# Two more places in a ring of split weights, paid with two of seven slab row buffers

## The chip, the cores and the metric

One core of one Trainium2 chip runs the whole program. The metric is the device time of one execution in microseconds, where lower is better. In the text PE is TensorE (PEld its weight loads), DVE is VectorE, ACT is ScalarE, POOL is GpSimd and SP is SyncE, which here only issues DMAs.

## The reference

Two decoder layers over 256 tokens of width 2048, in float32. Layer 0 mixes tokens by causal pooling and by attention to a memory of 256 tokens, layer 1 by differential attention over shared keys and values and by the same memory attention. Both end with a squared-ReLU feed-forward part (FFN) of width 8192, and these two FFNs are where the change acts:

```python
def squared_relu_mlp(h, w1, w2):
    z = jax.nn.relu(h @ w1)
    return (z * z) @ w2
...
        x = x + jnp.concatenate([token_out, mem_out], axis=-1) @ w_out[i]
        x = x + squared_relu_mlp(rms_norm(x, ffn_norm[i]), w_ff1[i], w_ff2[i])
```

## The kernel before, in words

The matmuls run in a rounded float32 format. To keep float32 accuracy every operand is split into a high part (the rounded value) and a low part (the rest), and a product is the sum of high times high, low times high and high times low. All weights (some 370 MB) pass through once: a DMA brings a row of 128x1024 from memory, ACT casts the high part (line 178), DVE subtracts it and gets the low part (line 181), and PE uses both. This supply is the class `Feed`.

The high and low parts lie in a ring of places of 512 columns: six in `hi_ring`/`lo_ring`, and during an FFN two more in the tile `slot` (`feed.extra`). `_slots` hands out one or two adjacent places and never goes across the end of a section, so a pair that does not fit skips a place. `fill(job)` prepares jobs up to `AHEAD` = 3 beyond the one that PE takes next, as long as places are free; `free(job)` returns them.

An FFN has two kinds of jobs. An up tile (64 a layer, `narrow`, lines 942 and 944) multiplies one column block of `w_ff1` into the single bank `x_bank`; it takes two plain rows (`R` jobs, two places each). The down product runs for half of its columns (A) and the other half (B) in 7 phases (`PHASES`), by a scheme with seven products in place of eight, whose seven PSUM banks are called `p`. It takes slabs, 58 a layer: a slab is two rows of `w_ff2`, to the first of which POOL adds part of the second by a summing DMA (line 149); DVE forms further sums in place (lines 209 and 212), and four jobs of 2, 1, 2 and 2 places come of it (`run`, lines 1033 to 1035, three matmuls for each place). `ffn_plan` mixes the two: up to two slab jobs ahead of an up tile for the first two tiles of a phase, then four or five. At a phase's end `finish_banks` takes the banks down on ACT and DVE, adds the sums of an earlier phase by a gather on POOL's queue (line 1089) or parks them in memory on SP's (line 1093). Eight last down tiles (`down_tile`) close the FFN.

Rows need buffers. Plain rows have four (`raw`). Slab rows have the three buffers `rows` and during an FFN also the room of the residual, whose four quarters are stored to memory first (`kept`, line 855): seven buffers in turn (`feed.more`). Quarters a and b are out of that turn from the next to last slab of phase 5 (the last B phase), c and d later. In phase 6 (the last A phase, the tail below) the residual comes back by `reload` (line 862): a and b after slab 23, c and d after slab 31.

In the tail there is more to do beside the slabs: the results of phase 5 are turned (transposes named `ct`) and added to the residual (line 1105), and in the end so are those of phase 6.

The instructions of each engine run in the order in which a scheduler has put them, which knows the places, the buffers and estimated durations. So a change of the ring also changes how casts, copies and DMAs stand in their queues.

Of the kernel before, what the change touches and what calls it, by code (L numbers as in the profile page):

```python
# [10 lines left out]
F32 = mybir.dt.float32  # L11
F32R = mybir.dt.float32r
# [6 lines left out]
P = 128  # L19
T = 256  # L20
# [6 lines left out]
SLOTS, AHEAD, LOADS, KOFF, RAWS = 6, 3, 3, 2, 4  # L27
# [78 lines left out]
class Feed:  # L106


    def __init__(self, tc, wst, wpool, rows, plan, dry):
        self.tc, self.nc, self.wst, self.wpool, self.rows = tc, tc.nc, wst, wpool, rows  # L110
        self.plan, self.dry = plan, dry
        self.pos = 0
        self.slab_no = 0
        self.lp = self.pp = 0
        self.raw = {}
        self.split = {}
        self.rows_whole = False
        self.extra = None
        self.more, self.lent, self.turn = [], {}, 0
        if not dry:  # L120
            self.hi = wpool.tile([P, SLOTS * 512], F32R, name="hi_ring")
            self.lo = wpool.tile([P, SLOTS * 512], F32R, name="lo_ring")
            self.busy = [False] * (SLOTS + 2)
            self.at = 0

    def load(self, upto):
# [26 lines left out]
            self.lp += 1  # L153

    def _slots(self, n):
        total = SLOTS + 2 if self.extra else SLOTS
        a = self.at
        if a < SLOTS < a + n:
            a = SLOTS
        if a + n > total:  # L160
            a = 0
        if any(self.busy[a : a + n]):
            return None
        for i in range(a, a + n):
            self.busy[i] = True
        self.at = a + n
        return a

    def _split(self, job, src, n):
        a = self._slots(n)  # L170
        if a is None:
            return False
        if a < SLOTS:
            hi, lo = self.hi[:, a * 512 : (a + n) * 512], self.lo[:, a * 512 : (a + n) * 512]
        else:
            c = (a - SLOTS) * 512
            hi, lo = (self.extra[:, b + c : b + c + n * 512] for b in (0, 1024))
        cast = self.nc.scalar.copy(hi, src)  # L178
        if self.pp < 2 or job[0] == "S" and job[2] == 0:
            self.tc.keep_in_program_order(cast)  # L180
        self.nc.vector.tensor_sub(lo, src, hi.bitcast(F32))  # L181
        self.split[job] = (hi, lo, range(a, a + n))
        return True
# [34 lines left out]

    def fill(self, job):
        i = self.plan.where[job]  # L220
        while self.pp < min(i + 1 + AHEAD, len(self.plan.prep)):
            if not self._prepare(self.plan.prep[self.pp]):
                assert self.pp > i
                break
            self.pp += 1
# [68 lines left out]
NB = 26  # L294
# [3 lines left out]
LAST = len(PHASES) - 1  # L298
# [67 lines left out]
def program(ctx, tc, plan, dry, xT, memT, par, lam, cst, wst, yT):  # L366
    nc = tc.nc
    cp = ctx.enter_context(tc.tile_pool(name="cp", bufs=1))
    sp = ctx.enter_context(tc.tile_pool(name="sp", bufs=1))
# [7 lines left out]
    feed = Feed(tc, wst, wp, tp, plan, dry)  # L377
# [7 lines left out]
    def at(d, fn, rank=0):  # L385
        pend.setdefault(now[0] + d, []).append((rank, fn))
# [33 lines left out]

    memraw = sp.tile([P, NK, T], F32, tag="S1", name="memraw")
    def resid_part(i, name):
        return sp.tile([P, 4, T], F32, tag=f"resid{i}", name=name)

    resid = Halves([resid_part(i, f"resid{i}") for i in "abcd"], 4)
    gmem = cp.tile([P, NK], F32, name="gmem")
    nc.scalar.dma_start(gmem, par[:, G_MEM : G_MEM + NK])

# [408 lines left out]
    def ffn(l, xs, tag, done):  # L837
# [7 lines left out]
        feed.extra = None if dry else sp.tile([P, 2048], F32R, tag="half", name=f"slot{l}")  # L845
# [7 lines left out]
        kept = dp.tile([P, NK, T], F32, tag="kept", name=f"kept{l}")  # L853
# [3 lines left out]
        def reload(tags):  # L857
            for i in tags:
                assert f"resid{i}" not in feed.lent.values()
                j = "abcd".index(i)  # L860
                resid.parts[j] = resid_part(i, f"resid{i}{l}")
                nc.sync.dma_start(resid.parts[j], kept[:, 4 * j : 4 * j + 4, :])

        feed.more = [] if dry else [(sp, f"resid{i}") for i in "abcd"]
        spare = list(range(len(spots)))
        zat, sat, due = {}, {}, {}

        def take():
            return spare.pop(0)
# [179 lines left out]
        def finish_banks(p):  # L1049

            half, begin, end = PHASES[p]
# [60 lines left out]
            if p == LAST:  # L1112
                for t, side in enumerate((upp, low)):
                    stt(
                        side, side, r2c[0][:, t : t + 1], fetched[t].bitcast(F32),
                        ALU.mult, ALU.add,
                    )
                for h in range(4):
                    at(7 + h, lambda h=h: turn(h))
                return  # L1120
            if old is not None:
                at(10, gather)
# [16 lines left out]
        ends = [None]  # L1139

        def go(some):
            for at_, what in some:
                if what[0] == "s":
                    p, i, j = what[1:]
                    if not banks:
                        open_banks()
                    if (p, i) not in runs:
                        runs[p, i] = slab_jobs(p, i)
                    runs[p, i](j)
                    if at_ < first_down and at_ >= ups:  # L1150
# [44 lines left out]
    half = sp.tile([P, 2048], F32R, tag="half", name="half0")  # L1195
# [295 lines left out]
    ab = [carve(384) for _ in range(2)]  # L1491
# [167 lines left out]
    for c in range(3):  # L1659
# [5 lines left out]
        for i in range(2):  # L1665
            j = 2 * c + i
# [127 lines left out]
```

## Time and profile before

| | |
|---|---|
| median of 3 runs | 2031.41 us (2030.1 to 2033.28) |
| the profiled execution's own time | 2031.04 us |
| its span, first to last instruction | 2029.3 us |
| granted PE clock | 1.000 of full speed |
| DMA | 453.43 MB, mean 223 GB/s |
| FFN of layer 0, FFN of layer 1 | from about 240 to 935 us, from about 1325 to 2025 us |

The two FFNs are over two thirds of the span. A group's row gives the line, the engine, what is written from what, how often, the busy time and the mean of one, and then the idle time of the engine just before, with what ended it. A row of the waits gives the engine and line that waited, the one waited for, and then the total in us, the number of waits and the longest. A row of the timeline gives start and duration in us. A row of the windows gives the stretch, its length, and the busy time of PE, PEld, DVE, ACT and POOL with the number of instructions, then the granted clock, the DMA engines' busy share and GB/s.

### The profile page before, as it was taken

The page shows a single profiled execution, that of the slowest core. Times are in us where ns is not written, and L with a number is a line of the kernel's source. Part 1 is how long each engine was busy: PE and PEld are TensorE (multiplying, and loading weights), DVE is VectorE, ACT ScalarE, POOL GpSimd, SP SyncE. Part 2 cuts the span into 40 slices and gives each one's busy share as a digit, 9 for nine tenths or more (in the row PEclk, how much of TensorE's full clock was granted, in tenths as well). Part 3 has the DMA queues.
Part 4 walks back from the last instruction along what each step waited for, and adds up shares of the span by engine and source line. Part 5 has one row for each costly group of instructions (what it writes and reads, how often), then busy time and mean ns, then how long its engine had stood idle before and what let it go on. Part 6 is the DMA issues. An engine that isn't in the chain of part 4 may idle for free.

```text
span 2029.3 us, 30490 instructions
## 1 busy us (share of the span) xinstructions
PE 2013.5 (99%) x10548; PEld 1695.9 (84%) x10548; DVE 1797.7 (89%) x2713; ACT 1376.7 (68%) x2213; POOL 175.0 (9%) x207
## 2 busy tenths in 40 slices
PE   9999999999999999999999999999999999999999
PEld 7888888888888888788888899888888888888877
DVE  8888779999999999999875798879999989898989
ACT  7765567666666676668665698566676667676764
POOL 0001300001011111000000000410001001010100
PEclk9999999999999999999999999999999999999999
DMA  9566767778788788765655645767877878786874
GB/s 309 181 199 214 238 202 246 243 219 262 221 237 261 238 244 235 239 190 194 222 185 191 194 141 181 237 225 230 238 229 223 263 223 269 214 265 214 260 205 156
DMA packets 139978, 453.43 MB, mean 223 GB/s; under 512 B 15856, under 2 KB 18928, under 8 KB 139824
## 3 DMA queue, kind: packets, MB, share of 16 engines
q1 hardware_dynamic: 119520, 412.68, 60.6%
q0 software_dynamic: 20160, 38.81, 11.5%
q8 instruction: 82, 1.34, 0.3%
q14 instruction: 72, 0.59, 0.1%
q10 hardware_dynamic: 144, 0.01, 0.0%
HBM read 431.90 MB, written 16.78 MB: 221 GB/s over the span
## 4 chain that ended last, share of the span: by engine, by line
PE 94%; DVE 3%; ACT 1%; issue 1%; DMA 1%; SPq 0%; DVEq 0%; ACTq 0%
PE x_bank L942 21%; PE x_bank L944 11%; PE p L1033 9%; PE p L1035 8%; PE p L1034 8%; PE wo L521 6%; PE wo L523 3%; PE ff L942 3%; PE q L552 3%; PE k L552 3%; PE v L552 3%; PE u L521 2%; PE mk L552 2%; PE mv L552 2%; PE ff L944 1%; DVE lo_ring L181 1%
## 5 line engine op out<-in xcount | busy, mean ns | idle before, releaser
L181 DVE TENSOR_TENSOR lo_ring<-raw,hi_ring 128x512 fp32r<-128x512 f32 (+1 forms) x657 | 551.8, 852 | 92.9 <-ACT hi_ring L178 86.7
L178 ACT CAST hi_ring<-raw 128x512 fp32r<-128x512 f32 (+1 forms) x657 | 480.4, 744 | 212.1 <-PE wo L521 62.3
L178 ACT CAST hi_ring<-slab 128x1024 fp32r<-128x1024 f32 (+1 forms) x350 | 312.9, 905 | 180.2 <-DVE slab L212 156.9
L181 DVE TENSOR_TENSOR lo_ring<-slab,hi_ring 128x1024 fp32r<-128x1024 f32 (+1 forms) x350 | 361.6, 1046 | 46.2 <-ACT hi_ring L178 44.6
L149 POOL DMA_DIRECT2D slab<-in_w x116 | 100.3, 865 | 1632.0 <-DVE rc L496 338.5
L942 PE MATMUL x_bank<-fx,hi_ring 128*128 128x512 f32 x688 | 218.7, 396 | 1.0 <-ACT hi_ring L178 0.9
L181 DVE TENSOR_TENSOR slot<-slab,slot 128x1024 fp32r<-128x1024 f32 x114 | 139.4, 1223 | 28.0 <-ACT slot L178 23.7
L521 PE MATMUL wo<-cat,hi_ring 128*128 128x512 f32 x512 | 161.7, 397 | 0.0
L944 PEld LDWEIGHTS x_bank<-fx,lo_ring 128*128 128x128 f32 x688 | 129.0, 188 | 30.8 <-DVE lo_ring L181 1.2
L178 ACT CAST slot<-slab 128x1024 fp32r<-128x1024 f32 x114 | 119.7, 1050 | 40.5 <-PE x_bank L942 31.5
L212 DVE TENSOR_TENSOR slab<-slab,slab 128x1024 f32<-128x1024 f32 x116 | 141.8, 1222 | 0.3
L944 PE MATMUL x_bank<-fx,lo_ring 128*128 128x256 f32 x688 | 136.2, 279 | 0.0
L942 PE MATMUL x_bank<-fx0b,hi_ring 128*128 128x512 f32 x384 | 120.7, 396 | 0.0
L523 PEld LDWEIGHTS wo<-cat,lo_ring 128*128 128x128 f32 x512 | 96.2, 188 | 21.9
L942 PEld LDWEIGHTS x_bank<-fx,hi_ring 128*128 128x128 f32 x688 | 107.9, 189 | 6.0 <-ACT hi_ring L178 2.1
L1033 PE MATMUL p<-hi_ring,zb 128*128 128x512 f32 x274 | 109.7, 401 | 1.3 <-ACT hi_ring L178 1.1
L1035 PE MATMUL p<-lo_ring,zb 128*128 128x512 f32 x274 | 106.2, 397 | 1.7 <-DVE lo_ring L181 1.7
L1034 PE MATMUL p<-hi_ring,zb 128*128 128x512 f32 x274 | 107.0, 392 | 0.0
L956 ACT COPY room<-x_bank 128x512 f32<-128x512 f32 x118 | 68.5, 580 | 49.6 <-PE x_bank L944 49.5
L523 PE MATMUL wo<-cat,lo_ring 128*128 128x256 f32 x512 | 101.8, 278 | 0.0
L942 PE MATMUL x_bank<-fx0a,hi_ring 128*128 128x512 f32 x304 | 97.7, 396 | 0.5 <-ACT hi_ring L178 0.2
L178 ACT CAST slot<-raw 128x1024 fp32r<-128x1024 f32 (+1 forms) x72 | 73.8, 1028 | 29.7 <-PE x_bank L942 16.5
(554 smaller groups left out, 4773.7 us busy)
## 6 DMA issues: line engine op xcount, KB each, us to landing
raw<-in_w SPq DMA_DIRECT2D x492, 512.0 KB, 4.5
slab<-in_w SPq DMA_DIRECT2D x232, 512.0 KB, 4.4
slab<-in_w POOLq DMA_DIRECT2D x116, 256.0 KB, 5.8
part<-room SPq DMA_DIRECT2D x10, 512.0 KB, 4.4
room<-part POOLq DMA_DIRECT2D x8, 512.0 KB, 10.1
part<-c_x SPq DMA_DIRECT2D x10, 256.0 KB, 5.6
part<-c_y SPq DMA_DIRECT2D x10, 256.0 KB, 4.6
c_x<-part POOLq DMA_DIRECT2D x8, 256.0 KB, 5.8
```

The source lines that it names most:

```text
L149: self.nc.gpsimd.dma_start(t[:, 512:1024], self.wst[other, :, 512:1024], accum_op=ALU.add)
L178: cast = self.nc.scalar.copy(hi, src)
L181: self.nc.vector.tensor_sub(lo, src, hi.bitcast(F32))
L212: add(two, t.unsqueeze(1).to_broadcast([P, 2, 512]), two)
L521: nc.tensor.matmul(ps, hi, xs[:, k, :], start=first and j == 0, stop=False)
L523: nc.tensor.matmul(ps[:, T : 2 * T], lo, xs[:, k, 0:T], start=False, stop=last and j == len(ks) - 1,)
L552: nc.tensor.matmul(ps[t], a, b, start=i == 0 and j == 0, stop=i == NK - 1 and j == 2)
L942: nc.tensor.matmul(ps, hi, src(k), start=k == ks[0], stop=False)
L944: nc.tensor.matmul(ps[:, T : 2 * T], lo, src(k)[:, 0:T], start=False, stop=k == ks[-1])
L1033: nc.tensor.matmul(ps, al, hi[:, s], start=i == begin, stop=False)
L1034: nc.tensor.matmul(ps, ah, hi[:, s], start=False, stop=False)
L1035: nc.tensor.matmul(ps, ah, lo[:, s], start=False, stop=i == end - 1)
```

## The change

The quarters a and b of the residual's room become one tile `resida`. In an FFN it is a second `slot` of two places, so the ring has ten. `ahead` is 5 during the FFN. Slab rows have the turn of `rows` and quarters c and d alone: five buffers. After slab 22 of phase 5 the new places are taken out of use again; a and b are reloaded after slab 22 of phase 6 (as two DMAs into one tile), the turn of c and d ends after slab 27 and not 28, and the turns at the very end of the FFN stand one tick later.

```diff
     def _slots(self, n):
-        total = SLOTS + 2 if self.extra else SLOTS
+        ends = range(SLOTS, SLOTS + 2 * len(self.extra) + 1, 2)
         a = self.at
-        if a < SLOTS < a + n:
-            a = SLOTS
-        if a + n > total:
+        for end in ends:
+            if a < end < a + n:
+                a = end
+        if a + n > ends[-1]:
             a = 0
...
-        while self.pp < min(i + 1 + AHEAD, len(self.plan.prep)):
+        while self.pp < min(i + 1 + self.ahead, len(self.plan.prep)):
...
     def resid_part(i, name):
-        return sp.tile([P, 4, T], F32, tag=f"resid{i}", name=name)
+        if i == "a":
+            both = sp.tile([P, 8, T], F32, tag="resida", name=name)
+            return [both[:, 0:4, :], both[:, 4:8, :]]
+        return [sp.tile([P, 4, T], F32, tag=f"resid{i}", name=name)]
...
-        feed.more = [] if dry else [(sp, f"resid{i}") for i in "abcd"]
+        feed.more = [] if dry else [(sp, f"resid{i}") for i in "cd"]
+        feed.ahead = 5
...
+        feed.extra = [] if dry else [
+            sp.tile([P, 2048], F32R, tag=tag, name=f"slot{l}") for tag in ("half", "resida")
+        ]
...
-                    at(7 + h, lambda h=h: turn(h))
+                    at(8 + h, lambda h=h: turn(h))
...
-                    if (p, i, j) == (LAST - 1, NB - 2, 3):
-                        feed.more = feed.more[2:]
-                    if (p, i, j) == (LAST, 23, 3):
-                        reload("ab")
-                    if (p, i, j) == (LAST, 28, 3):
+                    if (p, i, j) == (LAST - 1, 22, 3):
+                        del feed.extra[1:]
+                    if (p, i, j) == (LAST, 22, 3):
+                        assert dry or not any(feed.busy[SLOTS + 2 :])
+                        reload("a")
+                    if (p, i, j) == (LAST, 27, 3):
                         feed.more = []
...
                 if at_ == len(items) - 3:
-                    feed.extra = None
+                    feed.extra = []
+                    feed.ahead = AHEAD
```

How the instructions move, at two places. The number behind `raw` or `slab` is that of the weight row in the order of the stream; the last number only tells buffers apart. First ACT at the end of phase 2 in layer 0, from the copy of the first bank of that phase (`c_x<-p0`) to the copy of the up tile's bank (`x_bank`) and on. Before:

```order
L1066 COPY c_x_4498<-p0_3742 128x512
L925 CAST za0_2624<-room0_2626 128x512
L1067 COPY room0_2626<-p6_3748 128x512
L178 CAST hi_ring_76<-slab169_4360 128x1024
L178 CAST slot0_2627<-raw173_4472 128x1024
L178 CAST hi_ring_76<-raw174_4477 128x1024
L956 COPY room0_2626<-x_bank_4510 128x512
L178 CAST hi_ring_76<-slab169_4360 128x512
L178 CAST hi_ring_76<-slab170_4380 128x1024
```

And of the change at the same place:

```order
L1074 COPY c_x_4503<-p0_3746 128x512
L180 CAST hi_ring_76<-slab169_4350 128x1024
L180 CAST slot0_2631<-raw173_4447 128x1024
L1075 COPY room0_2625<-p6_3752 128x512
L180 CAST hi_ring_76<-slab169_4350 128x512
L180 CAST slot0_2632<-raw174_4468 128x1024
L180 CAST hi_ring_76<-slab170_4356 128x1024
L964 COPY room0_2625<-x_bank_4515 128x512
```

Two casts of slab rows that stood behind the copy of `x_bank` stand ahead of it. Next SP's queue in layer 0, at the reload of the residual's quarter a (b follows) shortly ahead of the tail. Before:

```order
L147 DMA slab300_7194<-in_w 128x1024
L147 DMA slab303_7274<-in_w 128x1024
L147 DMA raw297_7132<-in_w 128x1024
L147 DMA raw298_7170<-in_w 128x1024
L862 DMA resida0_7387<-kept0_2628 128x1024
L147 DMA raw301_7204<-in_w 128x1024
L147 DMA raw302_7272<-in_w 128x1024
L862 DMA residb0_7389<-kept0_2628 128x1024
```

And of the change, from the same reload on:

```order
L866 DMA resida0_7303<-kept0_2626 128x1024
L148 DMA slab287_6873<-in_w 128x1024
L148 DMA raw291_6956<-in_w 128x1024
L148 DMA slab289_6951<-in_w 128x1024
L148 DMA raw292_7032<-in_w 128x1024
L866 DMA resida0_7303<-kept0_2626 128x1024
L148 DMA slab290_6954<-in_w 128x1024
L148 DMA raw293_7034<-in_w 128x1024
L148 DMA raw294_7036<-in_w 128x1024
L148 DMA slab295_7046<-in_w 128x1024
```

The reload moves some ten weight rows ahead, and the slab rows stand less far ahead of the plain rows: 303 is issued ahead of 297 before, 295 behind 294 in the change.

More of the change, by code (lines that the diff above doesn't have):

```diff
@@ L117, in __init__ @@
         self.rows_whole = False
-        self.extra = None
+        self.extra = []
+        self.ahead = AHEAD
         self.more, self.lent, self.turn = [], {}, 0
@@ L122, in __init__ @@
             self.lo = wpool.tile([P, SLOTS * 512], F32R, name="lo_ring")
-            self.busy = [False] * (SLOTS + 2)
+            self.busy = [False] * (SLOTS + 4)
             self.at = 0
@@ L175, in _split @@
         else:
-            c = (a - SLOTS) * 512
-            hi, lo = (self.extra[:, b + c : b + c + n * 512] for b in (0, 1024))
+            which, c = divmod((a - SLOTS) * 512, 1024)
+            hi, lo = (self.extra[which][:, b + c : b + c + n * 512] for b in (0, 1024))
         cast = self.nc.scalar.copy(hi, src)
@@ L422, in resid_part @@
     def resid_part(i, name):
-        return sp.tile([P, 4, T], F32, tag=f"resid{i}", name=name)
-    resid = Halves([resid_part(i, f"resid{i}") for i in "abcd"], 4)
+        if i == "a":
+            both = sp.tile([P, 8, T], F32, tag="resida", name=name)
+            return [both[:, 0:4, :], both[:, 4:8, :]]
+        return [sp.tile([P, 4, T], F32, tag=f"resid{i}", name=name)]
+    resid = Halves([x for i in "acd" for x in resid_part(i, f"resid{i}")], 4)
     gmem = cp.tile([P, NK], F32, name="gmem")
@@ L844, in ffn @@
         room = sp.tile([P, 4096], F32, tag="big", name=f"room{l}")
-        feed.extra = None if dry else sp.tile([P, 2048], F32R, tag="half", name=f"slot{l}")
         feed.rows_whole = True
@@ L859, in reload @@
                 assert f"resid{i}" not in feed.lent.values()
-                j = "abcd".index(i)
-                resid.parts[j] = resid_part(i, f"resid{i}{l}")
-                nc.sync.dma_start(resid.parts[j], kept[:, 4 * j : 4 * j + 4, :])
-        feed.more = [] if dry else [(sp, f"resid{i}") for i in "abcd"]
+                for j, x in enumerate(resid_part(i, f"resid{i}{l}"), "abcd".index(i)):
+                    resid.parts[j] = x
+                    nc.sync.dma_start(x, kept[:, 4 * j : 4 * j + 4, :])
+        feed.more = [] if dry else [(sp, f"resid{i}") for i in "cd"]
+        feed.ahead = 5
         spare = list(range(len(spots)))
         zat, sat, due = {}, {}, {}
+        feed.extra = [] if dry else [
+            sp.tile([P, 2048], F32R, tag=tag, name=f"slot{l}") for tag in ("half", "resida")
+        ]
         def take():
```

## The prediction

> **What bounds the kernel now.** I read the head of the profile's page first, then the waits of the weight loads, then TensorE's timeline at one stop, and last the queues that feed it.
>
> ```profile
> span 2029.3 us, 30490 instructions
> PE 2013.5 (99%) x10548; PEld 1695.9 (84%) x10548; DVE 1797.7 (89%) x2713; ACT 1376.7 (68%) x2213; POOL 175.0 (9%) x207
> ```
>
> TensorE (PE) is busy for all but 15.8 us. A matmul's row lasts longer than the step to the next one, though, so short stops are swallowed. They show in the starts. A stretch of an up tile, a stop, and ScalarE (ACT) at that stop:
>
> ```profile
> 475.54 0.63 PE L942 MATMUL x_bank<-fx0a,slot 128*128 128x512 f32 x2
> 476.00 0.39 PE L944 MATMUL x_bank<-fx0a,slot 128*128 128x256 f32 x2
> 476.23 0.63 PE L942 MATMUL x_bank<-fx0a,slot 128*128 128x512 f32 x2
> ...
> 481.33 0.39 PE L1034 MATMUL p<-hi_ring,zb 128*128 128x512 f32 x1
> 481.56 0.39 PE L1035 MATMUL p<-lo_ring,zb 128*128 128x512 f32 x1
> 481.97 0.73 PE L942 MATMUL x_bank<-fx0a,slot 128*128 128x512 f32 x2
> 482.54 0.44 PE L1033 MATMUL p<-hi_ring,zb 128*128 128x512 f32 x1
> 482.82 0.40 PE L1034 MATMUL p<-hi_ring,zb 128*128 128x512 f32 x1
> 483.44 0.51 PE L1033 MATMUL p<-hi_ring,zb 128*128 128x512 f32 x1 [0.22 <-ACT hi_ring L178]
> 483.78 0.40 PE L944 MATMUL x_bank<-fx0a,slot 128*128 128x256 f32 x2
> ```
>
> ```profile
> 480.38 1.05 ACT L178 CAST hi_ring<-raw 128x1024 fp32r<-128x1024 f32 x1 [1.73 <-PE x_bank L942]
> 481.34 0.58 ACT L956 COPY room<-x_bank 128x512 f32<-128x512 f32 x1
> 481.81 1.57 ACT L178 CAST hi_ring<-slab 128x512 fp32r<-128x512 f32 x2
> ```
>
> Undisturbed, a slab matmul follows the last after 0.23 us and two blocks of an up tile take 0.69 us. At 482.82 the step is 0.62 and the next 0.34 us: 0.50 us lost, of which the row calls 0.22 idle. The cast that PE wanted stood behind the bank's copy, which had to wait for the up tile's end. The load of those weights has its own row, and all such waits are summed in the view of the waits:
>
> ```profile
> 483.43 0.19 PEld L1033 LDWEIGHTS p<-hi_ring,zb 128*128 128x128 f32 x1 [0.65 <-ACT hi_ring L178]
> ```
>
> ```profile
> PEld p L1033 <- ACT hi_ring L178: 16.8, 42, 0.7
> PEld p L1035 <- DVE lo_ring L181: 12.2, 37, 1.4
> ...
> PEld x_bank L944 <- DVE lo_ring L181: 4.4, 14, 1.5
> PEld x_bank L942 <- ACT hi_ring L178: 2.8, 4, 0.8
> PEld x_bank L944 <- DVE slot L181: 2.1, 6, 0.4
> PEld p L1035 <- DVE slot L181: 2.0, 9, 0.2
> ...
> PEld p L1033 <- ACT slot L178: 1.3, 1, 1.3
> ```
>
> These lines belong to the two feed-forward stages (FFN), and all wait for the high or low part of weights. They sum to 41.6 us in 113 waits. The sample waited 0.65 us and cost 0.50, so I take 0.15 off each: 41.6 - 113 x 0.15 = 24.6 us is all that a better supplied ring can win, 1.2% of the run.
>
> The Trainium skill (Perfetto Trace Analysis, Identifying the Most-Contended Engine) says that matmul busy time misleads and that the busy share of weight loads shows the headroom. By it the 84% above would leave 16%, over 300 us. The steps of 0.23 us show that most of that is not to be had by this change, and the sum goes by the waits.
>
> **The change part by part.** *Two more places, five ahead.* Counted through the ring's bookkeeping at the moment PE is done with a job: before, 6.3 of 8 places hold prepared weights on average over the slab jobs, since four prepared jobs rarely fill eight places. After, 9.0 of 10 do until slab 22 of the last B phase, then 7.1 of 8 (the last tile's room is given back, the five ahead stay). A tile of up work with one slab takes eleven places: four of 1.40 us (four blocks of 0.35) and seven of 0.68 us (three matmuls of 0.23), 10.4 us, so 0.94 us a place. PE's stock grows from 5.9 to 8.5 us, and to 6.7 us in the tail.
>
> The waits by stretch, first layer up to about where the places are given back; then the largest row of the same stretch of the second layer (1330 to 1840), which repeats it:
>
> ```profile
> PEld p L1033 <- ACT hi_ring L178: 5.7, 15, 0.7
> PEld p L1035 <- DVE lo_ring L181: 3.4, 13, 0.4
> ...
> PEld x_bank L944 <- DVE lo_ring L181: 1.0, 5, 0.2
> PEld p L1035 <- DVE slot L181: 0.7, 3, 0.2
> PEld x_bank L944 <- DVE slot L181: 0.7, 2, 0.4
> PEld x_bank L942 <- ACT hi_ring L178: 0.7, 1, 0.7
> ```
>
> ```profile
> PEld p L1033 <- ACT hi_ring L178: 5.7, 15, 0.7
> ```
>
> 12.2 us in 39 waits, 6.4 us lost; twice that is 12.8 us in the deep stretches. The tails hold the other 11.8 us. No deep wait is over 0.7 us, and the stops of one phase end add to about 1 us, against 2.6 us more stock: it could all go. What may keep some is VectorE (DVE), which makes the low parts:
>
> ```profile
> 630.00:680.00 50.00, 50.00 (x255) 41.53 (x255) 44.37 (x51) 32.15 (x41) 4.32 (x5) 1.00 0.76 220
> 680.00:730.00 50.00, 49.33 (x245) 39.58 (x244) 48.71 (x62) 36.65 (x48) 6.09 (x7) 1.00 0.87 262
> ```
>
> In the second window DVE (busy 48.71 of 50 us) is full to 97%, so nothing can be caught up there; in the first, 89%, a stock is refilled. I take 80%: -10.2 us (bounds 0 and -12.8). In the tails stock grows by 0.8 us against single waits of up to 1.5 us; I take 40%: -4.7 us (0 to -11.8).
>
> *Five row buffers for seven.* Here is the price. In the trace each slab load starts as a buffer comes free.
>
> ```profile
> L1033 PE MATMUL p<-hi_ring,za x155: 387/390/507, 282.3 to 917.3; 128*128 128x512 f32 x155
> ```
>
> ```profile
> raw<-in_w SPq DMA_DIRECT2D x492, 512.0 KB, 4.5
> slab<-in_w SPq DMA_DIRECT2D x232, 512.0 KB, 4.4
> slab<-in_w POOLq DMA_DIRECT2D x116, 256.0 KB, 5.8
> ...
> room<-part POOLq DMA_DIRECT2D x8, 512.0 KB, 10.1
> ```
>
> 58 slabs in 635 us are 10.9 us each. Seven buffers turn over in 3.5 slabs, 38 us; five in 27 us. Load and sum take 4.4 + 5.8 us and about 1 us to issue; a slab is held while it is split, some 7 us (seven of eleven places of the cycle). Of 38 us about 20 were slack; of 27 about 9 are left. On average that costs nothing, and its cover is that slack; behind a gather of partial sums (10.1 us on the same queue) it is used up, and the stock pays. I put 0, with the bad end in a rival.
>
> *Last slabs.* The two parked buffers now serve up to slab 54 and not 56, so slabs 56 and 57 take row buffers alone. Slab 56 waits for the buffer of slab 54, before for a parked one that slab 53 left: one slab, 10.9 us, later, some 2 us more than the slack, borne by a stock of 6.7 us that is the thinner for it. +1 us a layer, +2 us (0 to +8).
>
> *Parked residual.* Its first half comes back before the phase-end gather, not within it. What that costs now, from SP's queue and PE's timeline:
>
> ```profile
> 794.53 0.33 SPq L862 DMA_DIRECT2D resida<-kept  x1
> ...
> 807.39 0.33 SPq L862 DMA_DIRECT2D residb<-kept  x1
> ```
>
> ```profile
> 821.00 0.39 PE L944 MATMUL x_bank<-fx0a,lo_ring 128*128 128x256 f32 x1 [1.08 <-DVE lo_ring L181]
> ```
>
> This 1.1 us stop in the first layer follows the two reloads, which crowd the weights; it is in the tails' 40%. The second half is asked for ahead of the last slabs, where SP's queue then waits for the parked buffers; that is in the +2 us. The adds of the last turn, one tick later, end long before the last down tile: 0. The ring's new tile waits for the residual's store, issued early in both layers: 0.
>
> *Sum*, against the profiled execution's 2031.04 us (its span 2029.3 and 1.7 around it; the median of the runs, 2031.41, is 0.4 above): 2031.0 - 10.2 - 4.7 + 2 = 2018.1. I say 2018, 0.65% faster.
>
> **The rivals.** *DVE is the limit.* The stock grows, but what PE lacks is work of a saturated engine, and the waits only come later. For it: the 97% window, and 89% over the span. Against: 89% in the window before, where each lost microsecond can be made good. With 15% of 12.8 us gone and the tails unchanged: 2029. *The change does little of what it says*, since pairs that don't fit the end of a section waste a place: 2031; the count of 9.0 speaks against it.
>
> *Slower: the slab's sum comes late behind the gather.* The eight gathers hold POOL's queue 10.1 us and the slack is 9, less where a load is slow. From a lateness of 8.5 us beyond the slack on, PE stands. If each gather costs 2 us and the gain at phase ends, half of the deep one, is lost, 5.1 of it and the tails' 4.7 are left: 16 - 5.1 - 4.7 + 2 = 8.2 us more, 2039. For it: in the tail of the first layer, which already runs on five buffers, one such stop is the 1.1 us above. Against: the others there are not of slabs.
>
> *Slower: ACT is held by its own casts.* A full ring makes every cast wait for PE, as the one at 480.38 does, and the copy of the only up-tile bank stands behind it. In 28 tiles (two at each of seven phase starts, two layers) only two slab jobs, some 2 us, cover copy and casts; a slip of one cast, 1.05 us, in each would cost 29 us and end at 2047. In the new order no cast ahead of a copy needs a place that is freed later than that tile but for two, so it is unlikely. The Trainium skill (TensorE: Matmul & The Clock Gate, Architectural detail) bears on it: it calls the queues of ScalarE and VectorE strictly first in, first out, and the trace agrees with the copy and casts above.
>
> **How the numbers follow.** 0.2% is 4 us, about what a measurement of this kernel can tell from no change. Forecast 0.70 (2018; its own range goes from nine tenths of the 24.6 us gone to the edge of what can be told, 2009 to 2027). DVE-limited 0.13 and little done 0.03 are within 0.2%: 0.16. Late sums 0.10 and held casts 0.04 are slower: 0.14. The whole range goes from that 2009 to 2037, which leaves out most of the two slow cases.
>
> **What would show it.** Right: the 41.6 us of these waits fall to under 20, most in the deep stretches; the stop by 483 gone, DVE's busy time the same 1798 us in a shorter span. The tail's rows should shrink least. Wrong: deep waits that stay with DVE over 95% in every window (the limit); waits of ACT for a slab's sum from POOL, several us each near a gather (supply); weight loads that wait longer for the copy of the bank (held casts).

## The result, and the profile after

The changed kernel takes **2017.56 us** (median of 4 runs, 2016.01 to 2019.05) against 2031.97 us of the kernel before in the same comparison: ratio 0.993, 95% interval 0.9912 to 0.9947. It is faster by 0.7%, and 0.4 us off the predicted 2018. The terms of the sum were much further off than the sum, and this part is mostly about that.

The head of the page of the changed kernel's profile (its execution took 2016.46 us, 1.8 around the span):

```profile
span 2014.7 us, 30538 instructions
PE 1997.2 (99%) x10548; PEld 1703.3 (85%) x10548; DVE 1794.9 (89%) x2713; ACT 1382.8 (69%) x2213; POOL 175.8 (9%) x207
```

DVE's and ACT's work is the same in a shorter span, as it should be if only waits went. The weight loads' waits of the whole run (us in total, times, longest):

```profile
PEld x_bank L950 <- DVE za L922: 6.2, 1, 6.2
PEld p L1041 <- ACT hi_ring L180: 3.1, 7, 0.7
PEld p L1043 <- DVE slot L183: 2.7, 10, 0.5
PEld x_bank L950 <- ACT zb L918: 2.1, 2, 1.1
PEld p L1041 <- ACT slot L180: 1.9, 6, 0.7
...
PEld p L1043 <- DVE lo_ring L183: 1.7, 6, 0.5
...
PEld x_bank L952 <- DVE lo_ring L183: 1.5, 4, 0.8
```

Line numbers have moved by 8: L1041 and L1043 are the L1033 and L1035 of before. Added over all lines of the two FFN whose releaser is a high or low part of weights, 41.6 us in 113 waits have become 10.9 us in 33. But a line stands on top that before did not have: one wait of 6.2 us, for an operand of the activations (za) and not for weights.

The stretch that the prediction showed with its stop by 483 us now runs through, TensorE's timeline of the changed kernel:

```profile
479.87 0.40 PE L1041 MATMUL p<-hi_ring,zb 128*128 128x512 f32 x1
480.11 0.39 PE L1042 MATMUL p<-hi_ring,zb 128*128 128x512 f32 x1
480.34 0.39 PE L1043 MATMUL p<-lo_ring,zb 128*128 128x512 f32 x1
480.56 0.39 PE L1041 MATMUL p<-hi_ring,zb 128*128 128x512 f32 x1
```

Every step is 0.22 to 0.24 us. To see where the time went without any rule for the price of a wait, take fixed points of the program: the start of a slab's first matmul. Here are slabs 1, 44 and 57 (counted from 0, so 57 is the last) of the first layer and the same three of the second, kernel before:

```profile
296.83 0.40 PE L1033 MATMUL p<-slot,za 128*128 128x512 f32 x1
767.28 0.39 PE L1033 MATMUL p<-slot,zb 128*128 128x512 f32 x1
913.22 0.40 PE L1033 MATMUL p<-hi_ring,za 128*128 128x512 f32 x1
1381.47 0.40 PE L1033 MATMUL p<-slot,za1a 128*128 128x512 f32 x1
1851.94 0.39 PE L1033 MATMUL p<-slot,zb 128*128 128x512 f32 x1
1997.24 0.40 PE L1033 MATMUL p<-hi_ring,za1a 128*128 128x512 f32 x1
```

and the changed kernel:

```profile
297.39 0.40 PE L1041 MATMUL p<-slot,za 128*128 128x512 f32 x1
759.70 0.39 PE L1041 MATMUL p<-slot,zb 128*128 128x512 f32 x1
908.43 0.40 PE L1041 MATMUL p<-hi_ring,za 128*128 128x512 f32 x1
1377.04 0.40 PE L1041 MATMUL p<-slot,za1a 128*128 128x512 f32 x1
1838.65 0.39 PE L1041 MATMUL p<-hi_ring,zb 128*128 128x512 f32 x1
1982.03 0.40 PE L1041 MATMUL p<-slot,za1a 128*128 128x512 f32 x1
```

The differences of neighbouring rows, in us. The last column is an experiment below, put here to be compared:

| stretch | before | changed | difference | changed, parked buffers one slab longer |
|---|---|---|---|---|
| deep, first layer (slab 1 to 44) | 470.45 | 462.31 | -8.1 | 462.24 |
| tail, first layer (44 to 57) | 145.94 | 148.73 | **+2.8** | 141.10 |
| deep, second layer | 470.47 | 461.61 | -8.9 | 461.54 |
| tail, second layer | 145.30 | 143.38 | -1.9 | 143.36 |
| all else of the span | 797.1 | 798.7 | +1.5 | 799.7 |

So the deep stretches gave 17.0 us, and the first layer's tail lost 2.8 us, more than the second's won. That loss holds the new line of 6.2 us. TensorE there, in the changed kernel:

```profile
885.02 0.39 PE L1041 MATMUL p<-hi_ring,zb 128*128 128x512 f32 x1
891.31 1.22 PE L950 MATMUL x_bank<-za,slot 128*128 128x512 f32 x2 [5.90 <-DVE za L922]
...
893.19 0.63 PE L1043 MATMUL p<-lo_ring,zb 128*128 128x512 f32 x1
893.61 0.63 PE L1041 MATMUL p<-hi_ring,zb 128*128 128x512 f32 x1
```

The step from 885.02 to 891.31 is 6.29 us where 0.23 is usual: 6.1 us lost. Then the steps are 0.42 us for some 4 us. What za waited for is found one engine back. ACT's timeline, then POOL's:

```profile
887.62 1.04 ACT L180 CAST hi_ring<-slab 128x1024 fp32r<-128x1024 f32 x1 [5.90 <-DMA slab<-in_w]
888.57 0.62 ACT L913 ACTIVATE room<-room 128x512 f32<-128x512 f32 x1
```

```profile
880.39 0.86 POOL L150 DMA_DIRECT2D slab<-in_w  x1 [22.46 <-DVE slab L214]
```

ACT stood at the cast of slab 56, whose sum POOL had asked for at 880.39 and which came 7.2 us later. (POOL's row names a step of DVE that ended at 879.86. But the slab's load landed at 879.83, and here as in the kernel before and in the fourth and fifth experiment below POOL asks for the sum of slab 56 some 0.55 us after that landing: the load is what it waited for.) Behind that cast, in ACT's queue, stood the activation work (L913) that za comes from. DVE in turn idled 5.83 us on L913. The sum was late because the slab's load was late: SP issued it at 874.26 us, behind the reload of the parked residual. The buffer it goes to came free at 874.23, when DVE ended the last low part of slab 54, so it was the buffer and not the queue that SP waited for last. The changed kernel's SP queue, then its DVE:

```profile
870.30 0.33 SPq L866 DMA_DIRECT2D residd<-kept  x1
871.99 1.47 SPq L148 DMA_DIRECT2D raw<-in_w  x2
874.26 6.00 SPq L148 DMA_DIRECT2D slab<-in_w  x2
```

```profile
873.01 1.22 DVE L183 TENSOR_TENSOR slot<-slab,slot 128x1024 fp32r<-128x1024 f32 x1
```

### The profile page after: what moved, and what is told of

It reads as the page before. It is cut to its first block, busy times and chain, and to the rows that moved or that the text cites. A ratio compares the mean times of both kernels' runs of the same rounds, so it can differ in the third digit from the quotient of the medians.

```text
span 2014.7 us, 30538 instructions
## 1 busy us (share of the span) xinstructions
PE 1997.2 (99%) x10548; PEld 1703.3 (85%) x10548; DVE 1794.9 (89%) x2713; ACT 1382.8 (69%) x2213; POOL 175.8 (9%) x207
## 4 chain that ended last, share of the span: by engine, by line
PE 94%; DMA 2%; DVE 2%; ACT 1%; issue 1%; SPq 0%; DVEq 0%; ACTq 0%; POOLq 0%
PE x_bank L950 22%; PE x_bank L952 11%; PE p L1043 9%; PE p L1041 9%; PE p L1042 8%; PE wo L526 6%; PE q L557 3%; PE k L557 3%; PE v L557 3%; PE wo L528 3%; PE ff L950 3%; PE u L526 2%; PE mk L557 2%; PE mv L557 2%; DMA raw<-in_w 1%; PE ff L952 1%
## 5 line engine op out<-in xcount | busy, mean ns | idle before, releaser
L180 ACT CAST hi_ring<-raw 128x512 fp32r<-128x512 f32 (+1 forms) x613 | 438.7, 728 | 220.8 <-PE wo L526 62.3
L183 DVE TENSOR_TENSOR lo_ring<-raw,hi_ring 128x512 fp32r<-128x512 f32 (+1 forms) x613 | 501.7, 830 | 97.4 <-ACT hi_ring L180 93.0
L180 ACT CAST hi_ring<-slab 128x1024 fp32r<-128x1024 f32 (+1 forms) x304 | 279.6, 931 | 182.1 <-DVE slab L214 101.7
L183 DVE TENSOR_TENSOR lo_ring<-slab,hi_ring 128x1024 fp32r<-128x1024 f32 (+1 forms) x304 | 322.4, 1073 | 35.1 <-ACT hi_ring L180 34.4
L180 ACT CAST slot<-slab 128x1024 fp32r<-128x1024 f32 (+1 forms) x160 | 153.2, 963 | 80.4 <-DVE slab L214 51.6
L183 DVE TENSOR_TENSOR slot<-slab,slot 128x1024 fp32r<-128x1024 f32 (+1 forms) x160 | 177.0, 1113 | 24.2 <-ACT slot L180 23.1
L183 DVE TENSOR_TENSOR slot<-raw,slot 128x1024 fp32r<-128x1024 f32 (+1 forms) x116 | 134.8, 1165 | 8.2 <-ACT slot L180 7.9
L180 ACT CAST slot<-raw 128x1024 fp32r<-128x1024 f32 (+1 forms) x116 | 116.4, 1007 | 35.5 <-PE x_bank L950 8.2
L950 PE MATMUL x_bank<-fx,slot 128*128 128x512 f32 x336 | 105.4, 395 | 0.0
L1041 PE MATMUL p<-hi_ring,zb 128*128 128x512 f32 x239 | 94.1, 394 | 0.1
L1042 PE MATMUL p<-hi_ring,zb 128*128 128x512 f32 x239 | 93.9, 393 | 0.0
L1043 PE MATMUL p<-lo_ring,zb 128*128 128x512 f32 x239 | 93.3, 392 | 0.1
```

What stands on the lines that cost most here:

```text
L950: nc.tensor.matmul(ps, hi, src(k), start=k == ks[0], stop=False)
L1041: nc.tensor.matmul(ps, al, hi[:, s], start=i == begin, stop=False)
L1042: nc.tensor.matmul(ps, ah, hi[:, s], start=False, stop=False)
L1043: nc.tensor.matmul(ps, ah, lo[:, s], start=False, stop=i == end - 1)
```

## The experiments

Ratios are to the kernel before, run on the same chip in the same comparison, with 95% intervals. Each run changes either the kernel before or the changed kernel, as its words say.

**The places without the lookahead.**

```
-        feed.ahead = 5
+        feed.ahead = AHEAD
```

> The change with the lookahead left at three jobs (ten places, five row buffers, early residual, all else as changed). Counted in the ring's bookkeeping, three jobs fill 6.4 of the ten places in the deep stretches and 6.1 in the tails, against 6.3 and 6.1 before. Theory (the gain is PE's stock): nothing is won in the deep stretches, their waits stay at some 12 us in 39, and the last slabs still cost: 2031 + 6 = 2037 us, between 2031 and 2041. Rival (the places themselves win, because a job that finds the end of a section no longer waits): 2020 us.

2026.13 us, ratio 0.9968 (0.9956 to 0.9981). Below the whole range of the theory, and not as low as the rival; its five executions spread from 2019.97 to 2027.37. In the trace the deep waits fell to 5.4 us in 19 in the first layer and 7.8 in 23 in the second, where I had said that they would stay. So bookkeeping's count of reserved places (6.4 against 6.3) is not PE's stock. This run also has the new cost at the last slabs.

**The lookahead without the places.** In the kernel before:

```
-        while self.pp < min(i + 1 + AHEAD, len(self.plan.prep)):
+        while self.pp < min(i + 1 + self.ahead, len(self.plan.prep)):
...
+        feed.ahead = 5
```

> The kernel before with the lookahead of the FFN at five jobs and nothing else (eight places, seven row buffers). Counted: 7.05 of 8 places in the deep stretches for 6.3, 7.15 in the tails for 6.1. Theory (stock decides): the deep stretches gain in the ratio of places, 0.76 of the 2.7 that the change brings, so some 3.5 us of 12, and the tails 2 to 4: 2025 us, between 2021 and 2028. Rival 1 (eight places can't use it, both parts are needed): 2031. Rival 2 (the lookahead is all of it, since single waits are 0.7 us and 0.7 us of stock is added): 2018.

2021.82 us, ratio 0.9953 (0.9939 to 0.9966): at the good end of the theory. Deep waits 5.8 us in 22 and 6.0 in 23, half of before.

**Five row buffers alone.** In the kernel before:

```
-        feed.more = [] if dry else [(sp, f"resid{i}") for i in "abcd"]
+        feed.more = [] if dry else [(sp, f"resid{i}") for i in "cd"]
...
-                    if (p, i, j) == (LAST - 1, NB - 2, 3):
-                        feed.more = feed.more[2:]
```

> The kernel before with two of its four parked buffers never lent, so five row buffers from the start; ring, lookahead and the rest as before, and the last slabs have the same buffers as before. Theory (the term at 0): 2031.5 within 2 us, waits of the weight loads as before. Rival (a slab's sum comes late behind a gather): 2033 to 2039, with new waits of ACT for the sum from POOL near phase ends.

2034.78 us, ratio 1.0015 (1.0007 to 1.0024): a cost of about 3 us, less than a measurement of this kernel can tell well, but the interval excludes zero. It is outside the theory's range and at the low end of the rival's, and the waits rose to 44.1 us in 117. But what the rival named does not show: of ACT's waits between 300 and 900 us none is for a slab's sum; the only one for a DMA is 1.5 us for a plain row. By the fixed points of above the cost lies in the deep stretches (472.1 and 473.6 us for 470.5 twice); how it comes about stays open. The run changes one thing more than its words say: since a and b are never lent, the scheduler fetches them back ahead of the FFN (at 193 and 213 us in the first layer) and not in the tail.

**The parked buffers one slab longer.** In the changed kernel:

```
-                    if (p, i, j) == (LAST, 27, 3):
+                    if (p, i, j) == (LAST, 28, 3):
                         feed.more = []
```

> The changed kernel with the two parked row buffers lent until slab 28 of the last phase, as before the change, and not 27: slab 56 then gets parked buffers in the first layer. Theory (the stop of 6 us at 885 of the changed kernel is slab 56 waiting for the row buffer of slab 54): the stop goes, with the slow steps behind it 8.5 us: 2009 us, between 2007 and 2012. Rival (it is the reload of the parked residual that holds the queue of SyncE, 5.5 us in the trace, and that reload comes ahead of the last slabs in this kernel too): the stop stays or moves, 2015 to 2018.

**2009.03 us**, ratio 0.989 (0.9877 to 0.9904), 8.5 us faster than the changed kernel and the theory's number. It beats both kernels. The same six points in its trace:

```profile
296.98 0.40 PE L1041 MATMUL p<-slot,za 128*128 128x512 f32 x1
759.22 0.39 PE L1041 MATMUL p<-slot,zb 128*128 128x512 f32 x1
900.32 0.40 PE L1041 MATMUL p<-hi_ring,za 128*128 128x512 f32 x1
1370.48 0.40 PE L1041 MATMUL p<-slot,za1a 128*128 128x512 f32 x1
1832.02 0.39 PE L1041 MATMUL p<-hi_ring,zb 128*128 128x512 f32 x1
1975.38 0.40 PE L1041 MATMUL p<-slot,za1a 128*128 128x512 f32 x1
```

Of the four stretches only the first layer's tail differs from the changed kernel, by 7.6 us; the other three agree within 0.1 us. Slab 56 now takes a parked buffer, and its load starts at 863.81 (SP's queue of this run):

```profile
863.81 6.31 SPq L148 DMA_DIRECT2D slab<-in_w  x2
...
890.36 0.33 SPq L866 DMA_DIRECT2D residc<-kept  x1
```

The second row shows a fault in what I expected of the rival: the reload of the residual has not stayed ahead of the last slabs here, it moved behind them. So this run alone does not part the two explanations; the next does.

**The rotation.** In the changed kernel, for the first layer alone (the second layer gets the count back):

```
         feed.ahead = 5
+        feed.turn += (1, -1)[l]
```

> The changed kernel with one count moved: the rotation through the five row buffers starts one place later in the first layer, so that it stands there as in the second layer. Slab 56 then takes the buffer of slab 54's first row, which comes free when that slab's differences are added, and not that of its second row, which is held until the last low part. Nothing else moves. Theory (the stop of 6 us is this one buffer's turn): the sum of slab 56 lands some 5 us earlier, the stop shrinks to about 1 us, 2011 us, between 2009 and 2013. Rival (the queue of SyncE or the reload of the residual holds it): 2016 to 2019, the stop still there.

2010.27 us, ratio 0.9895 (0.9882 to 0.9909). SP's queue of this run:

```profile
864.21 0.33 SPq L866 DMA_DIRECT2D residd<-kept  x1
870.20 0.33 SPq L148 DMA_DIRECT2D slab<-in_w  x1
871.89 1.47 SPq L148 DMA_DIRECT2D raw<-in_w  x2
```

Here a reload does stand ahead of slab 56 and still the slab goes at 870.20, 4.1 us earlier than in the changed kernel, since its buffer came free with an earlier step of slab 54. The stop shrinks to 1.0 us. The cost was which buffer's turn it was; the second layer escaped it because its rotation stood one place further on. The other reload does come later here, and ACT's cast of slab 56 stands one place earlier in its queue, so a share of theirs in the 7 us is not quite excluded.

**The places alone, without the last slabs' stop.** Both the edit of the first run and `(LAST, 28, 3)`:

> The changed kernel with the lookahead at three jobs and the parked row buffers lent one slab longer: the places (with five row buffers) without the lookahead and without the last slabs' stop. In ScalarE's queue 2.2 places' worth more casts stand ahead of each bank copy than before; with the lookahead alone it is 0.1. Theory (places win by where the casts stand, apart from the lookahead): 2026 less the last slabs, some 5 us, 2021, between 2018 and 2024. Rival (the places alone gave the 5 us in the tails and the row buffers eat the rest): 2026.

2019.78 us, ratio 0.994 (0.9926 to 0.9953), within the theory's range: the places alone win 12 us, and by the medians the last slabs took 6 of them back in the first run.

**A lookahead of four** (`feed.ahead = 4`, with `(LAST, 28, 3)`):

> The changed kernel with the parked buffers one slab longer, and a lookahead of four jobs and not five: 7.9 of ten places reserved in the deep stretches, 9.0 with five, 6.4 with three. Theory (both parts count and the deep stretches are almost cured): 2012 us, 2009 to 2015, between the 2009 with five and the run with three. Rival (the fifth job is idle, four are enough): 2009. Rival 2 (only a ring that is full wins): within 2 us of the run with three.

2011.39 us, ratio 0.9901 (0.9888 to 0.9915). Its interval overlaps that of five, so the run can't part the theory from the first rival. The fifth job is worth some 2 us by the medians, and as much in the deep stretches of the two traces (926.0 us in sum for 923.8). The second rival is out.

**The lookahead alone with five buffers** (the second and third run's edits together):

> The kernel before with the lookahead at five jobs and five row buffers from the start (eight places). With the short stock five buffers cost 3.4 us. Theory (late rows are paid from PE's stock, and the longer lookahead has more of it): 2023 us, 1 us above the lookahead alone, 2021 to 2024. Rival (the price of the buffers is a delay of its own and adds): 2025.

2018.79 us, ratio 0.9939 (0.9927 to 0.9952). Five buffers cost nothing here: the run is rather below the one with seven (0.9953), with overlapping intervals. The rival falls, and the run ends 2 us under the theory's range: its 1 us does not show.

These runs make a square, all with five row buffers and the last slabs served as before (ratios to the kernel before):

| | lookahead 3 | lookahead 5 |
|---|---|---|
| eight places | 1.0015 | 0.9939 |
| ten places | 0.9940 | 0.9890 |

Either part alone is worth about 0.75% of the run, 15 us; the second on top of the first is worth 0.5%, 10 us. The rows differ in more than places: the residual's first half is fetched back ahead of the FFN in the upper row and in the tail in the lower one, where the adds of the last turn also stand one tick later. Neither acts in the deep stretches, and there the square has the same shape: 945.6 and 933.3 us for both layers in the upper row, 931.9 and 923.8 in the lower one.

**Why places win at a lookahead of three.** ACT's queue order, which the scheduler makes, gives a lead. Counted in that order, 2.2 places' worth more casts stand ahead of each copy of an up tile's bank in the deep stretches with ten places than with eight; the lookahead alone makes that 0.1. The copy must wait for PE's last matmul of the tile, and a cast behind it waits too. ACT's waits at that copy between 300 and 700 us, kernel before, then the places alone (without the stop), then the lookahead alone:

```profile
ACT room L956 <- PE x_bank L944: 19.5, 13, 2.4
```

```profile
ACT room L964 <- PE x_bank L952: 5.5, 7, 1.5
```

```profile
ACT room L958 <- PE x_bank L946: 21.7, 20, 2.4
```

If the order is the reason, ten places are worth nothing when casts may not move ahead of the copy. That can be tried: every cast of the FFN is pinned behind what the program issues ahead of it.

```
-        if self.pp < 2 or job[0] == "S" and job[2] == 0:
+        if self.pp < 2 or self.rows_whole or job[0] == "S" and job[2] == 0:
             self.tc.keep_in_program_order(cast)
```

*In the kernel before* (eight places, lookahead three, pinned):

> The kernel before, with every cast of the FFN pinned in ScalarE's queue behind what the program issues ahead of it (the scheduler may no longer move a cast ahead of a bank copy). Counted in the queue: 1.9 places' worth fewer casts stand ahead of each copy than in the kernel before. It is the control for the next run. Theory (the place of the casts in the queue sets the stock): slower, as much as 2.2 places more are faster: 2031 + 10 = 2041 us, 2035 to 2050. Rival (only the number of places counts): 2031 within 3.

2137.31 us, ratio 1.0517 (1.0502 to 1.0533). Slower, but by 106 us where I had said 10. The waits for weight parts doubled in number and nearly quadrupled in sum, to 156 us in 238, 114 us more, so the time went where the theory says; 82.8 of the 106 us are in the deep stretches. But the pin holds back more than the casts that would pass a copy, so its size is not the copy's alone. Nor is all of it waiting: the granted clock was 0.994 of full speed here for 1.000 before, which over a span of 2133.4 us is up to some 13 us (an estimate, as if TensorE had been busy all the time). Its waits at the copy in the same window:

```profile
ACT room L956 <- PE x_bank L944: 57.6, 31, 4.5
```

*With ten places*, lookahead three and the parked buffers one slab longer, pinned in the same way:

> The run with the places alone (ten places, five row buffers, lookahead three, parked buffers one slab longer), with the casts pinned in the same way: ten places, but 1.9 places' worth fewer casts ahead of each copy than in the kernel before, the same as in the pinned kernel before. Theory (the places win only because the scheduler can move casts ahead of the copy): no faster than the pinned kernel before, within 3 us of it. Rival (the places win as places, a cast waits less for PE to release one): 10 us faster than the pinned kernel before, as the places alone were 11.7 us faster than the kernel before.

2143.53 us, ratio 1.0551 (1.0529 to 1.0573). The two extra places win nothing: the run with them (and five row buffers) is 6 us slower, beyond the 3 us that the theory allowed, with intervals that just overlap. In the deep stretches the two pinned runs agree within 0.2 us in sum. Its waits at the copy are the same:

```profile
ACT room L964 <- PE x_bank L952: 57.4, 31, 4.5
```

The rival, by which places win as places, falls as far as a kernel so much slower can show it. *With ten places, lookahead five* and the parked buffers one slab longer, pinned:

> The changed kernel with the parked buffers one slab longer (2009 us), with the casts pinned: ring of ten places and lookahead of five as there, 9.0 places reserved as there, but 1 place's worth of casts more ahead of each copy than before the change and not 2.6. Theory (the place in the queue): between 2009 and 2031 in the ratio of 1 to 2.6, 2022 us, 2015 to 2026. Rival (what the bookkeeping reserves counts): 2009 within 3.

2027.64 us, ratio 0.998 (0.9971 to 0.999): 18.6 us slower than the same kernel unpinned, with the same 9.0 places reserved. So the reservation alone does not decide. It ends 1.6 us above the range that I gave, and the fixed points show why the ratio of 1 to 2.6 was the wrong measure: only 4.9 us of the loss are in the deep stretches, where the casts were counted, and 12.7 in the tails. In the deep stretches this run keeps 12.2 of the 17.1 us with 1 place's worth of casts more ahead of the copies for 2.6. There the place in the queue is not all either: asking early wins much of it even where casts can't pass. Against the pinned run with ten places and a lookahead of three it is 116 us faster. What the pin costs in the tails I have not followed up.

**The first half of the residual one slab later** (`(LAST, 23, 3)` for `(LAST, 22, 3)`, with the parked buffers one slab longer):

> The changed kernel with the parked buffers one slab longer (2009 us), with the first half of the parked residual asked for after slab 23 of the last phase, as before the change, and not 22. The prediction put the earlier reload at the 1.1 us of one stop, inside the tails' share. Theory (0 within what can be told): 2009 within 2 us. Rival (the reload crowds the weights at the phase end): 2011 to 2012, with a stop by 820 again.

2008.55 us, ratio 0.9884 (0.987 to 0.9899): no difference, but the run decides nothing. The scheduler put the reload where it had been: it is issued at 761.47 us, as it is at 761.46 without the edit, and in the two traces every engine has the same instructions in the same order. So this is a repeat of the 2009.03 us, and the theory and its rival stand untried.

## Why the prediction was right, and where its steps were not

- **What bounds the kernel.** Right: weights that come late to PE, and what is won is what PE no longer waits. But 24.6 us was not all that could be won: the deep stretches alone gave 17.0, over my bound of 12.8. Two steps failed there. The sum took only the lines whose releaser was a weight part, and left out a line that has the same cause. In the waits of the first layer's deep stretch of the kernel before (from 240 to 750 us; the second layer's, from 1330 to 1840, has the same row):

```profile
PEld x_bank L942 <- ACT room L956: 2.2, 7, 0.4
```

PE wants the bank and ACT has not copied it yet, for its queue is held by casts: 4.4 us in 14 waits over both layers, and 0.8 us in 3 for bank copies in the changed kernel. With them the deep waits went from 28.9 us in 92 to 3.9 us in 16. That is 25.0 us less for 17.0 us of time in 76 waits, so a wait's hidden part was about 0.105 us, if nothing else changed there, and not the 0.15 us of the one sample.
- **Two more places, five ahead, deep stretches: -10.2 us forecast, -17.0 measured.** Besides the bound, 80% was too low: the deep waits for weights fell from 24.5 us to 3.1, and the largest row left in the first layer's is

```profile
PEld p L1043 <- DVE slot L183: 1.2, 5, 0.3
```

The reason given for it, a stock that grows from 5.9 to 8.5 us, was the wrong quantity. I paired each slab job's last-made low part with the load that reads it: from the end of DVE's row to the start of PE's load the median was 1.3 us before, 2.1 with the lookahead alone, 2.7 with the places alone and 3.5 in the changed kernel (170 to 173 jobs of the first deep stretch). In this order the first layer's stretch gets shorter: 470.5, 466.1, 464.9 and 462.3 us. A price it is not: in the second layer the places alone take longer than the lookahead alone (467.0 for 466.1), and in the pinned kernel before the median is 1.2 us and the stretch takes 512.5. The places that the bookkeeping holds are asked for, not filled. ACT's queue has a large part in filling them, and there the two halves of the change work by different ways: the places let the scheduler put casts ahead of the copy, the lookahead asks for them earlier. The way in which the lookahead gains with eight places, where the casts stand no further ahead of the copies, I have not shown.
- **Tails: -4.7 us forecast.** Without the last slabs' stop they gave 4.8 and 1.9 us (table above), 6.8 together.
- **Last slabs: +2 us forecast, +7.6 in the first layer and 0.0 in the second.** The mechanism was the one written down: slab 56 takes the buffer of slab 54, and its load came 10.4 us later (874.26 for 863.81, where the parked buffers serve one slab longer) against the 10.9 forecast. The size failed twice. Its sum then landed 14.6 us later (887.6 for 873.0), since the load took 5.6 us for 4.4 and the sum 7.2 for 4.2. In that other run ACT came to the cast 7.5 us after the sum had landed, a slack near the 9 us of the prediction; the other 7 us reached ACT's queue. And the price was put on the weights of slab 56 alone, while the cast that waits for them holds ACT's whole queue, activations included, and PE's next tile with it. The 6.7 us of stock that were to bear the lateness are weights; za has no such stock (PE waits 0.3 us for it even in that other run). The layers differ by the rotation, which I had left out.
- **Five row buffers: 0 forecast.** 3 us with the old lookahead, so the average slack did not cover them there; nothing that can be measured with the new. That the bad cases are paid out of the longer lead fits this, but is only argued.
- **Residual reloaded earlier: 0** apart from one stop. Not measured: the run meant for it moved nothing. That the two reloads make the stop at 821 us fits another run, though its order differs there in more than that: with five row buffers alone no reload stands in that tail, the stop is gone, and the first layer's tail is 1.0 us shorter (145.0 for 145.9).
- **The sum.** Deep stretches 6.8 us better than forecast, tails 2.1 better, last slabs 5.6 worse, all else 1.5 worse, on the profiled execution: 2018.1 - 6.8 - 2.1 + 5.6 + 1.5 = 2016.3, and it took 2016.5. The 1.5 us of all else is not explained. The direction and the cause were forecast; that the number came out within 0.4 us was luck, since errors of opposite sign cancelled.
- **The rivals.** DVE is not the limit. In the two windows of the prediction, changed kernel:

```profile
630.00:680.00 50.00, 50.00 (x254) 42.35 (x253) 47.00 (x55) 35.73 (x45) 4.31 (x5) 1.00 0.75 226
680.00:730.00 50.00, 50.00 (x257) 41.96 (x256) 45.71 (x55) 35.16 (x46) 6.06 (x7) 1.00 0.91 266
```

DVE's 89% and 97% have become 94% and 91% (47.00 and 45.71 of 50 us) with PE busy all the time (47.45 and 46.06 with both windows put 5 us earlier, since the changed kernel is ahead): DVE's work is spread more evenly, which a 50 us window at 97% did not rule out. A slab's sum that comes late did occur and cost 7.6 us, but at the last slabs and for want of a buffer, not behind a gather. That ACT's queue is held by a cast is also what that stop is; I had put this rival at the up tiles' copies, for want of a place in the ring, and priced it at one cast, while here the cast waited for a slab's sum. The Trainium skill (TensorE: Matmul & The Clock Gate, Architectural detail) calls ScalarE's queue strictly first in, first out; the 5.90 us at 887.62, with the activation work right behind that cast, agree with it.

## What to carry to other kernels

More places in a ring can be worth no more than the order of the preparing engine's queue makes of them: look at what stands ahead of the work that must be early, above all a copy that waits for the consumer, and measure the lead from the trace instead of counting reservations. See in the trace that an edit moved what it was to move; a scheduler can put it back. When a pool of buffers shrinks, follow the last few users through the rotation one by one, since the average slack says nothing about them, and price a late one by everything behind it in the waiting engine's queue. When a forecast of a sum is right, check the terms by fixed points of the program; here 8.5 us still lay in one of them.

## What the runs showed of the hardware

The stop of 6.1 us cost more than itself. Windows of the changed kernel (PEclk is the column after POOL's):

```profile
870.00:885.00 15.00, 15.00 (x79) 12.42 (x78) 12.56 (x15) 7.44 (x11) 0.86 (x1) 1.00 0.71 207
885.00:891.30 6.30, 0.41 (x3) 0.10 (x1) 2.07 (x4) 2.60 (x4) 0.86 (x1) 0.81 0.40 139
891.30:895.30 4.00, 3.99 (x10) 3.24 (x11) 3.35 (x6) 2.73 (x5) 0.00 (x0) 0.50 0.30 55
895.30:900.00 4.70, 4.70 (x23) 3.89 (x22) 3.72 (x6) 3.33 (x6) 0.00 (x0) 0.95 0.35 126
```

The granted clock was 0.50 for the 4.0 us after the stop, and the steps of 0.42 us for 0.23 cost some 2.1 us more. If the clock had only the values 1.00 and 0.50 here, the other windows tell when it changed. The 0.81 over the 6.30 us window of the stop means 0.50 for its last 2.4 us, so it fell at about 888.9, some 3.5 us after the last matmul had ended (885.02 and 0.39 us). The 0.95 of the last window is another 0.5 us at half, so full speed came back at about 895.8, 4.5 us after the work had. The Trainium skill (TensorE: Matmul & The Clock Gate, What's actually happening) puts the clock at half after an idle window of about 3.4 us or more and back to full after about 3.4 us or more of sustained work; the 3.5 and 4.5 us of this trace agree with both. This stop thus cost a third more than its own time.
